# The low half of each split weight chunk, made by a negation and an accumulating transfer

## The chip, the core and the metric

The kernel runs on one core of one Trainium2 chip. The metric is the device time of one execution in microseconds (us). The engines are TensorE (PE in the rows, its weight loads PEld), VectorE (DVE), ScalarE (ACT), GpSimd (POOL) and SyncE (SP, which here issues every transfer); 16 DMA engines move the data.

## The reference, cut to what matters

Two layers of a decoder trunk over 512 tokens of width 1024. Each layer is a token mixer (an input projection, three parallel mixers A, B and C, their projections, sigmoid gates, an output projection), a cross-attention into 256 memory tokens, and a SwiGLU FFN of hidden width 2816, each followed by a LayerNorm of the scaled residual sum:

```python
for l in range(DEPTH):
    h = hybrid_mixer(x, l, w_in[l], ..., w_br_a[l], w_br_b[l], w_br_c[l], w_out[l])
    x = layer_norm(DEEPNORM_ALPHA * x + h, ln1_g[l], ln1_b[l])
    x = layer_norm(DEEPNORM_ALPHA * x + memory_cross_attention(x, mem, xq[l], xkv[l], xo[l]), ...)
    x = layer_norm(DEEPNORM_ALPHA * x + swiglu(x, w_up[l], w_down[l]), ln3_g[l], ln3_b[l])
```

All weights and activations are float32. Nearly all the work is products of activations with the weight matrices.

## The kernel before, in words

**Split products.** A float32 operand w is split into a high part, w rounded to the type float32r (`whi`), and a low part, w minus the high part (`wlo`). A product is three matmuls, high by high, high by low and low by high, added up in PSUM.

**Chunks.** The weights lie in HBM as 372 chunks of 128 x 1024 floats (512 KB), in the order of use. `load_raw` (L254) has SyncE load a chunk into a `raw` tile; `split_chunk` (L262) has ScalarE cast it to `whi` (L267) and notes the subtraction in the list `late`; `flush` (L272) writes the noted subtractions `wlo = raw - whi` (L274), on VectorE for 347 chunks and on GpSimd for the 24 in `on_pool` (the key half of `xkv`, and the first two column tiles of each half of `w_up`), and then loads raw chunks until three more than were split are under way. Chunk 0 is split apart, at the start.

**Steps.** `make_program` lays down 376 steps. A tile step ("a") uses one chunk of 8 x 128 weight columns against all 512 tokens: 24 matmuls. A group ("b") uses several chunks at once for 128 tokens: four steps (two for `xkv`) that share four to six chunks, all of which the group's first step reads one after the other. The main loop (L923) writes, for each step: `refill` (at most two chunks are split, as long as fewer than `pairs` split chunks are live), any chunk of this step that is still unsplit, a `flush` where one is needed, the evacuation of the step before, a piece of the side work (`advance`: attention, recurrence, LayerNorm items), the step's matmuls, and a `flush`. `pairs` is 3 for most tile steps, 5 to 7 for groups and the FFN.

**Order and buffers.** The schedule is manual: every engine works through its instructions in the order in which this loop writes them, and waits on semaphores. `whi`, `wlo`, `raw` and most large activations share 39 slots of 4 KB per partition (`a4`), so a new tile waits for the readers of the tile that had its slot.

**Side work on GpSimd** that this text speaks of: the rotary products (L570, L571), the recurrence's low parts `xl` (L517, L518) and `bl` (L560), its product `ti` (L550), the merges `acc` (L631), and the powers (L376, L477) that give the reciprocal deviations of the norms.

Of the kernel before, what the change touches and what calls it, by code (L numbers as in the profile page):

```python
# [13 lines left out]
AF = mybir.ActivationFunctionType  # L14
ALU = mybir.AluOpType
# [38 lines left out]


def make_program():
    """Order of the matrix products: the weight chunks and the steps that use them.

    A chunk is [128, 1024] floats: (weight, layer, first row tile, row tiles, first column, columns).
    """  # L60
    chunks, steps = [], []

    def ch(name, l, k0, nk, c0, nc_):
# [3 lines left out]
    def tile_step(name, l, c0, act, post, n0=0, n1=S, **kw):  # L67
        c = ch(name, l, 0, KT, c0, P)
        st = Step("a", [c], act=act, post=post, nk=KT, ncol=P, off=0, n0=n0, n1=n1, **kw)
        steps.append(st)  # L70
        return st
# [11 lines left out]
    for l in range(L):  # L83
# [39 lines left out]
        for n in range(KT):  # L123
            st = tile_step("w_in", l, OFF_RX + P * n, "x", ("rx", l, n))
# [49 lines left out]
def kernel(  # L174
# [12 lines left out]
):  # L187
    nc = tc.nc
    chunks, steps = make_program()
    NCH = len(chunks)  # L190

# [10 lines left out]
    def a4(s, shape, dt=F32):  # L202
        return big.tile([P] + shape, dt, tag="a4", name=nm(s), bufs=39)
# [16 lines left out]
    V, A, G, T = nc.vector, nc.scalar, nc.gpsimd, nc.tensor  # L220
# [22 lines left out]
    for s, st in enumerate(steps):  # L243
        for c in st.chunks:
            last_use[c] = s
            if first_use[c] is None:
                first_use[c] = s
    on_pool = {c for c, (name, l, k0, nk, c0, n) in enumerate(chunks)
               if (name == "xkv" and c0 < D) or (name == "w_up" and c0 % HID < 2 * P)}
    raws, hi, lo, late = {}, {}, {}, []  # L250
    ptr = {"raw": 0, "split": 0}
    RAW_AHEAD = 3

    def load_raw():  # L254
        c = ptr["raw"]
        if c >= NCH:
            return
        raws[c] = a4("raw", [1024])
        nc.sync.dma_start(raws[c], wts[c])
        ptr["raw"] += 1  # L260

    def split_chunk(s):  # L262
        c = ptr["split"]
        while ptr["raw"] <= c:
            load_raw()
        h, lw, raw = a4("whi", [1024], F32R), a4("wlo", [1024], F32R), raws.pop(c)
        A.copy(h, raw)  # L267
        hi[c], lo[c] = h, lw
        late.append((lw, raw, h, G if c in on_pool else V))
        ptr["split"] += 1  # L270

    def flush():  # L272
        for lw, raw, h, eng in late:
            eng.tensor_tensor(lw, raw, f(h), ALU.subtract)  # L274
        late.clear()
        while ptr["raw"] < min(NCH, ptr["split"] + RAW_AHEAD):
            load_raw()

    def refill(s, pairs, limit):
        n = 0  # L280
        while ptr["split"] < NCH and n < limit:
            done = sum(1 for c in hi if last_use[c] <= s)
            if len(hi) - done >= pairs:
                break
            split_chunk(min(s, len(steps) - 1))
            n += 1
        for c in [c for c in hi if last_use[c] <= s]:
            del hi[c], lo[c]
# [14 lines left out]
    def met(k):  # L303
        return done.get(k, 0) >= goals.get(k, 1)
# [8 lines left out]
    def advance():  # L313
        for g in list(active):
            if not step_side(g):
                active.remove(g)
        n = 1 if not queue or queue[0][0] != "x" else 4 if len(queue) > 2 else 2
        for _ in range(min(n, len(queue))):
            if queue:
                g = queue.pop(0)[1]  # L320
                if step_side(g):
                    active.append(g)
        active.extend(fresh)
        fresh.clear()
        queue.extend(arriving)
        arriving.clear()
# [537 lines left out]
    for k in range(2):  # L864
        c = slice(512 * k, 512 * (k + 1))
# [8 lines left out]
    def setup_params():  # L874
        nc.sync.dma_start(cols, cols_in.rearrange("l p c -> p l c"))
        lq = t2("lq")
        nc.sync.dma_start(lq, lam_in.partition_broadcast(P))
        for t in range(NT):
            nc.sync.dma_start(x_res[t], x_in[t * P:(t + 1) * P, :])
        for l in range(L):  # L880
            A.activation(hb[:, l, :], cols[:, l, 40:56], AF.Copy, scale=0.5)
            li = 0.8 - 0.6 * math.exp(-0.3 * l)
            V.tensor_scalar(gain[:, l:l + 1], cols[:, l, 64:65], 1.0 - li, None, ALU.mult)
        s1 = small("s1")
        pr = t2("lp")
        for l in range(L):
            o = l * 256
            V.tensor_tensor(pr[:, o:o + 64], lq[:, o:o + 64], lq[:, o + 64:o + 128], ALU.mult)
            V.tensor_tensor(pr[:, o + 64:o + 128], lq[:, o + 128:o + 192], lq[:, o + 192:o + 256],
                            ALU.mult)  # L890
            V.tensor_reduce(s1[:, 2 * l:2 * l + 2],
                            pr[:, o:o + 128].rearrange("p (a b) -> p a b", a=2),
                            axis=AX.X, op=ALU.add)
        A.activation(s1[:, 4:8], s1[:, 0:4], AF.Exp)
        for l in range(L):
            li = 0.8 - 0.6 * math.exp(-0.3 * l)
            V.scalar_tensor_tensor(neglam[:, l:l + 1], s1[:, 5 + 2 * l:6 + 2 * l], -li,
                                   s1[:, 4 + 2 * l:5 + 2 * l], ALU.add, ALU.subtract)

    def setup_decay():  # L900
        s1, e, z, acc = small("s1"), small("e"), small("z"), small("acc")
        lam = cols[:, :, 56:64]
        zz, ee, aa = (t.rearrange("p (l n) -> p l n", l=2) for t in (z, e, acc))
        V.tensor_scalar(zz, lam, -1.0, None, ALU.mult)
        V.tensor_tensor(aa, zz, lam, ALU.max)
        A.activation(e, acc, AF.Exp, scale=-1.0)
        V.tensor_scalar(acc, e, 2.0, None, ALU.add)
        V.reciprocal(acc, acc)
        V.tensor_tensor(e, e, acc, ALU.mult)
        V.tensor_tensor(s1, e, e, ALU.mult)  # L910
        V.tensor_scalar(acc, s1, 1.0 / 21.0, None, ALU.mult)
        for k in range(9, 0, -1):
            V.scalar_tensor_tensor(acc, acc, 1.0 / (2 * k + 1), s1, ALU.add, ALU.mult)
        V.scalar_tensor_tensor(acc, acc, 1.0, e, ALU.add, ALU.mult)
        V.tensor_scalar(z, z, 0.0, 4.0, ALU.max, ALU.mult)
        fl = sp4.rearrange("p l n -> p (l n)")
        V.scalar_tensor_tensor(fl, acc, 8.0, z, ALU.mult, ALU.add)
        V.tensor_scalar(nsp4.rearrange("p l n -> p (l n)"), fl, -1.0, None, ALU.mult)
# [4 lines left out]
    for s, st in enumerate(steps):  # L923
        if s:
            refill(s - 1, steps[s - 1].pairs, 2)
        while ptr["split"] <= max(st.chunks):
            split_chunk(s)
        if late and ptr["split"] - len(late) <= max(st.chunks):
            flush()
        if prev is not None and prev[0].post:  # L930
            POST[prev[0].post[0]](prev[1], *prev[0].post[1:])
        if s == 3:
            setup_params()
        if s == 20:
            setup_decay()
        if st.pre:
            PRE[st.pre[0]](*st.pre[1:])
        credit += prev[0].cost() if prev else 1.0
        if credit > 0.75:
            advance()  # L940
            credit = 0.0
        while not all(met(k) for k in st.need):
            assert active or queue or fresh or arriving, (s, st.need)
            advance()
        prev = (st, emit_main(st))
        flush()
# [26 lines left out]
def _layout(inp):  # L973
    inp = {k: np.asarray(v) for k, v in inp.items()}
    chunks, _ = make_program()
    wts = np.empty((len(chunks), P, 1024), np.float32)
    for i, (name, l, k0, nk, c0, ncol) in enumerate(chunks):
# [46 lines left out]
```

## Time and profile before

| | us |
|---|---|
| median of 2 runs (2271.61 to 2272.38) | 2271.99 |
| the profiled execution: its span | 2272.3 |
| PE busy | 2238.5 (99%) |
| DVE busy | 1267.1 (56%) |
| ACT busy | 898.3 (40%) |
| POOL busy | 351.6 (15%) |
| DMA: share of 16 engines' span, transfers by SP | 29.5% |

The span runs from the first instruction to the last on the core. A PE row lasts longer than its place in the stream, since matmuls overlap: a 128x512 one is shown with 0.39 us and the next starts 0.23 us later, so the busy share alone doesn't tell how full the stream is. The waits say that: idle time of an engine by what ended it. PEclk is the TensorE clock granted in a stretch, as a share of full speed.

### The profile page before, as it was taken

The numbers are of one execution on the slowest core, as the hardware profiler recorded it, in microseconds if no ns is written. First come the engines' busy times: TensorE is split into PE (matmuls) and PEld (weight loads), VectorE is DVE, ScalarE is ACT, GpSimd is POOL, SyncE is SP. The second block draws the span as 40 slices with busy tenths as digits, with TensorE's granted clock in tenths as the row PEclk, the third lists the DMA queues.
The fourth block names the chain that finished last, engine by engine and source line by source line (L and its number), as shares of the span: only waits on it lengthen the run. The fifth ranks groups of instructions, "written<-read, shape, count | busy, mean of one in ns | idle before, by whom it ended". The sixth has DMA issues, their size and how long they took to land.

```text
span 2272.3 us, 26789 instructions
## 1 busy us (share of the span) xinstructions
PE 2238.5 (99%) x10516; PEld 1821.5 (80%) x10516; DVE 1267.1 (56%) x2058; ACT 898.3 (40%) x1583; POOL 351.6 (15%) x238
## 2 busy tenths in 40 slices
PE   9999999999999999999999999999999999999998
PEld 7778777778888888888887777777788888888887
DVE  6656766646655743243566476666467457332434
ACT  5444466644244332122134445666432342221330
POOL 2202213320300300000022031133203003000000
PEclk9999999999999999999999999999999999999999
DMA  7122323234332222142231222232343323222321
GB/s 269 63 65 76 101 66 97 93 98 166 102 112 102 93 91 86 66 147 100 81 126 56 65 75 93 65 107 84 116 148 105 110 101 103 85 82 97 125 93 38
DMA packets 65278, 224.37 MB, mean 99 GB/s; under 512 B 7936, under 2 KB 7936, under 8 KB 65152
## 3 DMA queue, kind: packets, MB, share of 16 engines
q1 hardware_dynamic: 65152, 222.66, 29.5%
q8 instruction: 83, 1.36, 0.2%
q14 instruction: 43, 0.35, 0.0%
HBM read 212.14 MB, written 2.10 MB: 94 GB/s over the span
## 4 chain that ended last, share of the span: by engine, by line
PE 72%; issue 17%; DVE 5%; POOL 3%; ACT 2%; DMA 0%; SPq 0%; POOLq 0%; ACTq 0%
PE ps L810 17%; PE ps L811 17%; PE ps L812 17%; PE ps L839 5%; PE ps L841 5%; PE ps L840 5%; POOL wlo L274 2%; PE sc L341 2%; PE o L414 1%; PE sc L340 1%; DVE x L482 1%; POOL ln L477 1%; PE tp L408 1%; PE o L370 1%; ACT whi L267 1%
## 5 line engine op out<-in xcount | busy, mean ns | idle before, releaser
L810 PE MATMUL ps<-xh,whi 128*128 128x512 f32 (+1 forms) x1792 | 697.3, 389 | 2.9 <-ACT xh L868 1.7
L811 PE MATMUL ps<-xl,whi 128*128 128x512 f32 (+1 forms) x1792 | 689.1, 385 | 0.8 <-DVE xl L754 0.5
L812 PE MATMUL ps<-xh,wlo 128*128 128x512 f32 (+1 forms) x1792 | 688.2, 384 | 1.3 <-POOL wlo L274 1.3
L274 DVE TENSOR_TENSOR wlo<-raw,whi 128x1024 fp32r<-128x1024 f32 x347 | 447.3, 1303 | 47.7 <-ACT whi L267 40.2
L267 ACT CAST whi<-raw 128x1024 fp32r<-128x1024 f32 x371 | 382.7, 1046 | 148.9 <-PE ps L840 97.8
L810 PEld LDWEIGHTS ps<-xh,whi 128*128 128x128 f32 x1792 | 339.4, 189 | 80.7 <-issue 6.5
L812 PEld LDWEIGHTS ps<-xh,wlo 128*128 128x128 f32 x1792 | 339.2, 189 | 68.9 <-POOL wlo L274 2.1
L811 PEld LDWEIGHTS ps<-xl,whi 128*128 128x128 f32 x1792 | 339.5, 189 | 66.1 <-DVE xl L869 1.0
L477 POOL TENSOR_TENSOR ln<-ln,expo 128x1 f32<-128x1 f32 x24 | 34.4, 1434 | 1082.9 <-DVE ln L476 1082.9
L839 PE MATMUL ps<-whi,hh 128*128 128x512 f32 x352 | 137.1, 389 | 0.0
L841 PE MATMUL ps<-whi,hl 128*128 128x512 f32 x352 | 137.0, 389 | 0.0
L840 PE MATMUL ps<-wlo,hh 128*128 128x512 f32 x352 | 136.9, 389 | 0.0
L744 ACT CAST hh<-fg 128x512 fp32r<-128x512 f32 x44 | 27.3, 620 | 191.8 <-DVE fg L743 191.8
L501 ACT CAST xh<-tp 128x256 fp32r<-128x256 f32 x80 | 28.0, 376 | 178.4 <-PE tp L495 101.2
L733 DVE SCALAR_TENSOR_TENSOR fg<-fg,ps 128x512 f32<-128x512 f32 x44 | 30.3, 688 | 116.9 <-ACT fg L732 116.9
L743 DVE TENSOR_TENSOR fg<-fg,ps 128x512 f32<-128x512 f32 x44 | 30.3, 688 | 114.4 <-PE ps L812 114.4
L570 POOL TENSOR_TENSOR raw<-raw,tabs 128x512 f32<-128x512 f32 x32 | 42.6, 1332 | 250.6 <-ACT raw L567 250.6
L732 ACT ACTIVATE fg<-ps 128x512 f32<-128x512 f32 x44 | 26.3, 598 | 135.2 <-PE ps L812 135.2
L680 DVE SCALAR_TENSOR_TENSOR x<-ps,x 128x512 f32<-128x512 f32 x48 | 33.0, 686 | 80.5 <-PE ps L841 80.4
L274 POOL TENSOR_TENSOR wlo<-raw,whi 128x1024 fp32r<-128x1024 f32 x24 | 63.5, 2661 | 88.4 <-ACT whi L267 88.4
L840 PEld LDWEIGHTS ps<-wlo,hh 128*128 128x128 f32 x352 | 66.1, 188 | 13.7
L839 PEld LDWEIGHTS ps<-whi,hh 128*128 128x128 f32 x352 | 66.1, 188 | 13.7
(233 smaller groups left out, 3576.6 us busy)
## 6 DMA issues: line engine op xcount, KB each, us to landing
raw<-in_wts_dram SPq DMA_DIRECT2D x371, 512.0 KB, 3.6
xs<-xs SPq DMA_DIRECT2D x32, 128.0 KB, 2.2
lng<-in_lnp_in_dram SPq DMA_DIRECT2D x6, 512.0 KB, 4.7
lnb<-in_lnp_in_dram SPq DMA_DIRECT2D x6, 512.0 KB, 5.0
tabs<-in_tabs_in_dram SPq DMA_DIRECT2D x4, 512.0 KB, 8.5
x<-in_x_in_dram SPq DMA_DIRECT2D x4, 512.0 KB, 9.3
qkA<-qkA SPq DMA_DIRECT2D x16, 128.0 KB, 2.2
qkC<-qkC SPq DMA_DIRECT2D x16, 128.0 KB, 2.2
```

Source lines behind the costliest of these rows:

```text
L267: A.copy(h, raw)
L274: eng.tensor_tensor(lw, raw, f(h), ALU.subtract)
L341: T.matmul(sc[:, :w], ql[r, i * P:(i + 1) * P], kk[r, c, :w], start=False, stop=True)
L477: G.tensor_tensor(st[:, 15:16], st[:, 14:15], expo, ALU.pow)
L570: G.tensor_tensor(raw, raw, tab[:, 0, :], ALU.mult)
L680: V.scalar_tensor_tensor(xs, ps, co, xs, ALU.mult, ALU.add)
L810: T.matmul(pv, wh, xh, start=(kt == 0), stop=False)
L811: T.matmul(pv, wh, xl, start=False, stop=False)
L812: T.matmul(pv, wl, xh, start=False, stop=(kt == st.nk - 1))
L839: T.matmul(ps, xh, wh, start=(i == 0), stop=False)
L840: T.matmul(ps, xh, wl, start=False, stop=False)
L841: T.matmul(ps, xl, wh, start=False, stop=(i == n - 1))
```

## The change

For every chunk but the first eight and the 24 in `on_pool`, the subtraction on VectorE goes. In its place ScalarE writes the negated raw chunk, rounded to float32r, into `wlo` (which is -`whi`, as the rounding is symmetric), and GpSimd issues a transfer that reads the chunk once more from HBM and adds it to `wlo` in SBUF. Both are written in `split_chunk`, right behind the cast, so they stand ahead of what the loop writes next. The subtractions that stay go through `late` as before, but any that is noted is flushed in the same step, before the step's matmuls. The blank lines replace a docstring and shift later lines by four.

```diff
@@ -266,8 +266,12 @@
         h, lw, raw = a4("whi", [1024], F32R), a4("wlo", [1024], F32R), raws.pop(c)
         A.copy(h, raw)
         hi[c], lo[c] = h, lw
-        late.append((lw, raw, h, G if c in on_pool else V))
         ptr["split"] += 1
+        if c < 8 or c in on_pool:
+            late.append((lw, raw, h, G if c in on_pool else V))
+        else:
+            A.activation(lw, raw, AF.Copy, scale=-1.0)
+            nc.gpsimd.dma_start(lw, wts[c], accum_op=ALU.add)
@@ -925,7 +929,7 @@
         while ptr["split"] <= max(st.chunks):
             split_chunk(s)
-        if late and ptr["split"] - len(late) <= max(st.chunks):
+        if late:
             flush()
```

Counted over the program, VectorE loses 340 instructions, ScalarE gains 340 and GpSimd 340 transfers; TensorE's and SyncE's instructions are as many as before.

ScalarE, where the chunks of the first `w_out` group of layer 0 are split (`mh` is the high part of the merged branches, `mkh` of the memory keys). Before:

```order
L267 CAST whi_4507<-raw_4433 128x1024
L638 CAST mh_4475<-acc_2211 128x512
L267 CAST whi_4542<-raw_4468 128x1024
L267 CAST whi_4545<-raw_4505 128x1024
L707 CAST mkh_4548<-ps_4514 128x256
L267 CAST whi_4585<-raw_4540 128x1024
```

and now:

```order
L267 CAST whi_4579<-raw_4505 128x1024
L273 ACTIVATE wlo_4580<-raw_4505 128x1024
L642 CAST mh_4550<-acc_2240 128x512
L267 CAST whi_4615<-raw_4511 128x1024
L273 ACTIVATE wlo_4616<-raw_4511 128x1024
L267 CAST whi_4620<-raw_4546 128x1024
L273 ACTIVATE wlo_4621<-raw_4546 128x1024
L711 CAST mkh_4625<-ps_4588 128x256
L267 CAST whi_4660<-raw_4613 128x1024
L273 ACTIVATE wlo_4661<-raw_4613 128x1024
```

Each cast of a chunk is followed by its negation, and the casts behind it stand one instruction later for each.

GpSimd, at the last recurrence item of layer 0 that TensorE waits for (`xl` is the low part of its convolved input). Before:

```order
L631 TENSOR_TENSOR acc_2211<-acc_2211,g_3598 128x512 x2
L560 TENSOR_TENSOR bl_3340<-m_3522,bh_3339 128x512 x2
L517 TENSOR_TENSOR xl_3916<-xc_3809,xs_3874 64x512
L518 TENSOR_TENSOR xl_3916<-xc_3809,xs_3874 64x512
```

and now:

```order
L274 DMA wlo_3915<-in_wts_dram 128x1024
L635 TENSOR_TENSOR acc_2240<-acc_2240,g_3651 128x512
L274 DMA wlo_3967<-in_wts_dram 128x1024
L635 TENSOR_TENSOR acc_2240<-acc_2240,g_3651 128x512
L564 TENSOR_TENSOR bl_3387<-m_3573,bh_3386 128x512 x2
L521 TENSOR_TENSOR xl_3976<-xc_3867,xs_3933 64x512
L522 TENSOR_TENSOR xl_3976<-xc_3867,xs_3933 64x512
```

A transfer stands ahead of each merge, so the low parts behind them come after two transfers that wait for ScalarE's negations.

GpSimd, at the LayerNorm behind `w_out` of layer 0 (L477, now L481, are its powers; the subtractions are those of `xkv`). Before:

```order
L477 TENSOR_TENSOR ln_4624<-ln_4624,expo 128x1
L274 TENSOR_TENSOR wlo_4759<-raw_4724,whi_4758 128x1024
L477 TENSOR_TENSOR ln_4656<-ln_4656,expo 128x1
L477 TENSOR_TENSOR ln_4684<-ln_4684,expo 128x1
L477 TENSOR_TENSOR ln_4730<-ln_4730,expo 128x1
L274 TENSOR_TENSOR wlo_4861<-raw_4726,whi_4860 128x1024
L274 TENSOR_TENSOR wlo_4864<-raw_4728,whi_4863 128x1024
```

and now:

```order
L274 DMA wlo_4800<-in_wts_dram 128x1024
L278 TENSOR_TENSOR wlo_4839<-raw_4832,whi_4838 128x1024
L481 TENSOR_TENSOR ln_4701<-ln_4701,expo 128x1
L481 TENSOR_TENSOR ln_4733<-ln_4733,expo 128x1
L481 TENSOR_TENSOR ln_4761<-ln_4761,expo 128x1
L278 TENSOR_TENSOR wlo_4941<-raw_4834,whi_4940 128x1024
L278 TENSOR_TENSOR wlo_4944<-raw_4836,whi_4943 128x1024
L481 TENSOR_TENSOR ln_4804<-ln_4804,expo 128x1
```

The subtractions have moved ahead of the first and of the fourth power.

## Rows read from the trace of the kernel before

**Rows 1.** The page's head and its list of busy times.
```profile
span 2272.3 us, 26789 instructions
PE 2238.5 (99%) x10516; PEld 1821.5 (80%) x10516; DVE 1267.1 (56%) x2058; ACT 898.3 (40%) x1583; POOL 351.6 (15%) x238
```

**Rows 2.** Waits of PE: us in total, times, longest us.
```profile
PE z L525 <- POOL xl L517: 5.4, 2, 2.7
PE ps L812 <- POOL wlo L274: 5.1, 6, 1.9
PE tp L364 <- DVE pr L359: 4.4, 3, 3.3
PE tp L495 <- DVE x L482: 3.1, 2, 1.5
...
PE ps L811 <- DVE xl L869: 0.2, 1, 0.2
```

**Rows 3.** Groups by line: busy us, mean ns of one, idle before and releasers.
```profile
L274 DVE TENSOR_TENSOR wlo<-raw,whi 128x1024 fp32r<-128x1024 f32 x347 | 447.3, 1303 | 47.7 <-ACT whi L267 40.2 <-PE ps L841 7.4
L267 ACT CAST whi<-raw 128x1024 fp32r<-128x1024 f32 x371 | 382.7, 1046 | 148.9 <-PE ps L840 97.8 <-DVE wlo L274 26.8 <-DMA raw<-in_wts_dram 23.5
L546 ACT ACTIVATE m<-m 128x1024 f32<-128x1024 f32 x8 | 8.5, 1061 | 0.1
L570 POOL TENSOR_TENSOR raw<-raw,tabs 128x512 f32<-128x512 f32 x32 | 42.6, 1332 | 250.6 <-ACT raw L567 250.6
L274 POOL TENSOR_TENSOR wlo<-raw,whi 128x1024 fp32r<-128x1024 f32 x24 | 63.5, 2661 | 88.4 <-ACT whi L267 88.4
```

**Rows 4.** DMA queues; issues by line with KB each and median us to landing.
```profile
q1 hardware_dynamic: 65152, 222.66, 29.5%
raw<-in_wts_dram SPq DMA_DIRECT2D x371, 512.0 KB, 3.6
```

**Rows 5.** Timeline of SP: one issue (start us, us).
```profile
60.13 0.33 SPq L259 DMA_DIRECT2D raw<-in_wts_dram  x1
```

**Rows 6.** Stretches: PE, PEld, DVE, ACT, POOL busy, PEclk, DMA share, GB/s.
```profile
985.00:1078.00 93.00, 93.00 (x412) 77.02 (x411) 37.66 (x43) 26.42 (x34) 0.00 (x0) 1.00 0.28 96
555.00:575.00 20.00, 20.00 (x112) 17.52 (x112) 11.28 (x14) 8.97 (x12) 0.00 (x0) 1.00 0.60 210
618.00:648.00 30.00, 30.00 (x171) 26.36 (x171) 19.07 (x28) 15.95 (x28) 3.27 (x2) 1.00 0.42 141
1134.00:1148.00 14.00, 14.00 (x72) 11.76 (x71) 10.81 (x16) 6.30 (x13) 1.52 (x1) 1.00 0.65 235
466.00:476.00 10.00, 7.28 (x17) 4.79 (x17) 3.64 (x4) 4.35 (x6) 4.10 (x3) 0.66 0.42 134
```

**Rows 7.** Timeline of ACT: casts for the first `w_out` group.
```profile
554.07 1.05 ACT L267 CAST whi<-raw 128x1024 fp32r<-128x1024 f32 x1
...
556.99 1.99 ACT L267 CAST whi<-raw 128x1024 fp32r<-128x1024 f32 x2
558.88 0.36 ACT L707 CAST mkh<-ps 128x256 fp32r<-128x256 f32 x1
559.15 2.00 ACT L267 CAST whi<-raw 128x1024 fp32r<-128x1024 f32 x2
```

**Rows 8.** Timeline of PE: first use of that group's first and fourth `wlo`.
```profile
560.80 0.40 PE L840 MATMUL ps<-wlo,mh 128*128 128x512 f32 x1
...
564.90 0.39 PE L840 MATMUL ps<-wlo,mh 128*128 128x512 f32 x1
```

**Rows 9.** Timeline of ACT: casts for the second `xkv` value group.
```profile
633.16 2.95 ACT L267 CAST whi<-raw 128x1024 fp32r<-128x1024 f32 x3
```

**Rows 10.** Timeline of PE: first use of that group's fourth `wlo`.
```profile
642.23 0.39 PE L840 MATMUL ps<-wlo,mh 128*128 128x512 f32 x1
```

**Rows 11.** Timeline of ACT: last two casts for layer 1's first group.
```profile
1133.44 2.00 ACT L267 CAST whi<-raw 128x1024 fp32r<-128x1024 f32 x2
```

**Rows 12.** Timeline of PE: first use of that group's fourth `wlo`.
```profile
1139.55 0.39 PE L840 MATMUL ps<-wlo,xh 128*128 128x512 f32 x1
```

**Rows 13.** Timeline of ACT and POOL before the last recurrence item; PE's wait.
```profile
460.43 1.06 ACT L267 CAST whi<-raw 128x1024 fp32r<-128x1024 f32 x1
...
461.31 1.67 POOL L631 TENSOR_TENSOR acc<-acc,g 128x512 f32<-128x512 f32 x1 [1.09 <-DVE g L630]
...
468.89 0.79 PE L525 MATMUL z<-xl,gw 64*128 64x512 f32 x1 [2.72 <-POOL xl L517]
```

## The prediction

> **What bounds the kernel now.** I began with the head of the page and the busy times [rows 1]: TensorE is busy for 99% of a span of 2272.3 us, VectorE for 56%, ScalarE for 40%, GpSimd for 15%. A busy TensorE need not have a full stream, so the list of its waits came second [rows 2]. It has twelve entries, of which the first four and the last are shown, and they add up to 25.3 us. In the FFN the stream is simply full: 412 matmuls in 93.00 us are 0.226 us each [rows 6], and a tile step of 24 takes 5.42 us. So this kernel is bound by TensorE's stream, and what the change takes off VectorE, 340 subtractions at 1.303 us or 443 us [rows 3], lies almost wholly beside it. The ceiling of any gain is the 25.3 us of waits plus what half-speed stretches behind them cost. One of these shows in the ten microseconds from 466: TensorE waited 2.72 us [rows 13], then the granted clock averaged 0.66, that is, it had fallen from 2.4 to 1.2 GHz for 6.8 us, which costs 3.4 us of stream. The longest waits in the rows are 3.3 us, twice 2.7 us and 1.9 us [rows 2]; were all four followed by such a stretch, that is 14 us, so the ceiling is near 39 us, 1.7% of the span. About 2%, or 45 us, is what I take a measurement to tell from no change, so faster by that much is practically excluded.
>
> What can be lost is another matter, since `wlo` now comes later. The question is where a chunk's cast ends only a few microseconds before TensorE first reads its `wlo`.
>
> **The new path, step by step.** Before, `wlo` follows its cast by one subtraction of 1.30 us on an engine that is free half the time. Now:
> - The negation on ScalarE: 1.06 us, by the 128x1024 activation with a scale [rows 3]. 340 of them are 361 us, which lifts ScalarE to 55%. In a burst each cast also waits for the negations ahead of it.
> - The issue on GpSimd. The trace has none. Below, SyncE's 0.33 us [rows 5]; above, GpSimd's longest instruction, 2.66 us [rows 3]. I take 1.3 us, the mean of its short product [rows 3], as the price of one instruction on that engine. 340 of them are 442 us, GpSimd 35% busy.
> - From issue to landing. A raw load of the same 512 KB lands after 3.6 us (median) [rows 4]; that is the lower end. The DMA engines' time for one load is 0.295 x 2272.3 us x 0.524 MB / 222.66 MB = 1.58 us [rows 1, 4]. The accumulate must read the old `wlo` too, one more pass of the same bytes, so 5.2 us is the upper end. I take the middle, 4.4 us.
> - The DMA engines' time for one accumulate: 1.58 us at least, 3.16 us if the second read costs as much as the first. I take 2.0 us, nearer the plain load, since only the read from SBUF is new. 340 of them add 680 us to the 670 us now used, 59% of the span.
>
> Cast to landing is then 1.06 + 1.3 + 4.4 = 6.8 us. In a tile stage with three live pairs a chunk is split two steps ahead, about 10.8 us; in the FFN with six pairs, five steps, 27 us. Both cover 6.8 us, and per step of 5.42 us the DMA engines do 1.58 + 2.0 us. So the bulk of the chunks costs nothing; the cover is gone only if the accumulate holds the engines for more than 5.42 - 1.58 = 3.84 us.
>
> The bursts are different: a group's first step reads all its chunks in 5.4 us.
> - `w_out`, once per layer. Before, the four casts start at 554.07, 556.99 (two) and 559.15 [rows 7], the reads of the first and fourth `wlo` at 560.80 and 564.90 [rows 8]. With negations between them the fourth negation ends near 563.3. Plus 1.3 + 4.4 us is 569.0, 4.1 us late. The DMA engines are 60% busy in this stretch [rows 6]; four accumulates are 8 us, and about 6 us of loads come between, so from 557.5 the fourth lands near 572: 7 us late. Bounds: 563.3 + 0.33 + 3.6 is 2.3 us late; four at 3.16 us behind 8 us of loads, 15 us late.
> - The `xkv` value groups, once per layer, eight chunks for two token steps each. The last three casts start at 633.16 [rows 9]; with negations they end near 639.5, plus 5.7 is 645.2 against the read at 642.23 [rows 10]: 3 us. Eight accumulates are 16 us and the loads 42% of 30 us [rows 6], together 28.6 us where some 25 us are to be had: 3 us more, so 6. Bounds: 1 and 14 us.
> - Layer 1's first group. Two casts start at 1133.44 [rows 11]; the second negation ends at 1137.7, plus 5.7 is 1143.4 against 1139.55 [rows 12]: 4 us. Bounds 2 and, with engines 65% busy [rows 6], 9 us.
>
> Together 2 x (7 + 6) + 4 = 30 us, between 9 and 67. Some of these waits are as long as the 2.72 us behind which the clock fell; five more such stretches at 2 us net (half of 3.4 us and a little more, since at half speed the late chunk catches up) are 10 us, between 0 and 17.
>
> **What else moves.** GpSimd's queue gets a transfer ahead of each merge. Before the last recurrence item, the cast ends at 461.49 and its negation now at 462.5, while the merge behind the transfer started at 461.31 [rows 13]: 1.2 us of blocking and 1.3 us of issue, which delay `xl`, for which TensorE already waits. Twice, 5 us; between 0 and 10. Earlier items are blocked too, but TensorE doesn't wait for them.
>
> On the other side, subtractions of `on_pool` chunks now stand ahead of powers that wait for VectorE, so the 5.1 us that TensorE waits for `wlo` of GpSimd [rows 2] should mostly go. A VectorE with 443 us less to do should end most of the 4.4 us for `pr` [rows 2]. I take 9 us off, between 5 and the whole 39.
>
> The sum: 30 + 10 + 5 - 9 = +36 us on the profiled span of 2272.3 us, which is 0.3 us from the median of the runs: **2308 us**, 1.6% slower.
>
> **Rivals.** *The accumulate takes the engines twice as long as a load.* A result needs two reads, and if the two take turns it costs 3.16 us: then the bursts queue, and the places above are at their upper ends. 67 + 17 + 10 - 5 = +89 us, 2361 us, slower by 4%. It decides from about 2.3 us per accumulate, where the sum passes 45 us. For it speaks that loads already fill 42 to 65% of the bursts [rows 6]; against it that the second read is of SBUF and not of HBM. The Trainium skill's page "Collectives: The Full Stack", section "The bandwidth ceiling: the fold count and why AG ≠ RS ≠ AR", says that a reducing step is half as fast as a plain copy, because two source reads go through the same ring. No run shown so far has an accumulating transfer, so the trace neither agrees nor disagrees; by that rule the sum would be this rival's 2361 us.
>
> *The DMA engines become the bound.* From 3.84 us per accumulate the tile stages fall behind too. At 6 us each step of 5.42 us would need 7.6 us; over 340 chunks some 740 us, so about 3010 us, and at 4.5 us some 225 us, about 2500. Nothing in the trace shows such a price, only that the operation is unknown.
>
> *It is all hidden, and VectorE's relief shows.* If the transfers land within the bounds' lower ends, 9 us of bursts stand against 9 us or more of relief: 2272 us, and down to 2250 if most waits and half-speed stretches go. For it: most chunks have 10 us or more of lead. Against it: in the bursts even the lower ends are late.
>
> **Chances.** My forecast, bursts late by some tens of microseconds but within 2%: 0.45. Engines twice as long: 0.32. DMA-bound: 0.10. Hidden: 0.13. So faster by over 2% 0.01, within 2% 0.57, slower 0.42. The range leaves out the DMA-bound case and the better half of the hidden one: 2260 to 2375.
>
> **What would show it.** In the changed profile, TensorE should wait for transfers into `wlo` at L844 (`w_out`, `xkv` values, layer 1's first group) and hardly at L816; the waits for GpSimd's `wlo` should be gone and that for `xl` be longer. The row of the accumulates gives issue, landing and engine share: about 1.3 us, 4.4 us and 2.0 us. TensorE waiting for `wlo` in the FFN, or a DMA share far above 60%, would make the forecast wrong towards slower; no waits at the bursts, towards no change.

## The result and the profile after

The changed kernel takes 2387.28 us (median of two runs, 2381.02 and 2393.55) against 2271.99: a ratio of 1.0505, 95% interval 1.0475 to 1.0534. It is slower by 5%. The two runs lie 12.5 us apart with granted clocks of 0.977 and 0.970, and the trace is of the shorter one: the accounts below are of its 107 us, while the medians differ by 115. The forecast was 2308 and the range ended at 2375, so the time lies beyond it, on the side of the rival in which an accumulate takes the engines twice as long.

First the page's head, its DMA queues and its rows of DMA issues, for the profiled run of 2381.02 us. They answer to [rows 1, 4].

```profile
span 2379.2 us, 27760 instructions
PE 2272.6 (96%) x10516; PEld 1837.0 (77%) x10516; DVE 862.9 (36%) x1718; ACT 1219.0 (51%) x1923; POOL 612.7 (26%) x578
...
q0 software_dynamic: 48960, 178.28, 42.2%
q1 hardware_dynamic: 65152, 222.66, 27.6%
...
raw<-in_wts_dram SPq DMA_DIRECT2D x371, 512.0 KB, 5.5
...
wlo<-in_wts_dram POOLq DMA_DIRECT2D x340, 512.0 KB, 7.3
```

The last row is the new operation: an accumulate of 512 KB lands 7.3 us after its issue, where I had taken 4.4 and held 5.2 for the most. The queue q0 carries nothing but these 340 transfers, so each holds the 16 DMA engines for 0.422 x 2379.2 / 340 = 2.95 us, where I had taken 2.0. The raw loads suffer with it: 5.5 us instead of 3.6.

Next TensorE's waits, which answer to [rows 2]; the columns are the same.

```profile
PE ps L844 <- DMA wlo<-in_wts_dram: 60.9, 27, 6.6
PE tp L368 <- DVE pr L363: 10.5, 5, 4.1
PE z L529 <- POOL xl L521: 5.4, 2, 2.7
...
PE z L528 <- DMA xs<-xs: 3.9, 2, 2.0
...
PE ps L816 <- POOL wlo L278: 2.7, 2, 1.3
```

One new row heads the list, at the line that the forecast named: 27 waits at L844 for a transfer into `wlo`, 60.9 us. The fifteen rows of the list come to 98.1 us, 72.8 more than before. The rest is clock. The mean granted clock fell from 0.991 to 0.977; the time that this costs, span times the missing share, rose from 0.009 x 2272.3 = 20.5 to 0.023 x 2379.2 = 54.7 us, by 34. Together that is 107 us, and the span grew by 106.9. The clocks are rounded to 0.001, or 2 us of span, so the match is in part luck; but no other loss of more than a few microseconds is left. TensorE stands, and after standing it runs slowly for a while.

The groups by line, which answer to [rows 3]:

```profile
L267 ACT CAST whi<-raw 128x1024 fp32r<-128x1024 f32 x371 | 385.9, 1042 | 47.1 <-DMA raw<-in_wts_dram 43.5 <-PE ps L845 2.7
L273 ACT ACTIVATE wlo<-raw 128x1024 fp32r<-128x1024 f32 x340 | 358.9, 1056 | 84.3 <-PE ps L844 84.3
L274 POOL DMA_DIRECT2D wlo<-in_wts_dram x340 | 296.6, 872 | 1424.1 <-ACT wlo L273 1266.4 <-PE ps L816 36.4 <-PE ps L845 18.9
```

The negation costs 1.056 us, as taken. The issue costs 0.87 us on GpSimd, less than the 1.3 taken. The long idle time before L274 is GpSimd waiting at the head of its queue for negations: 1266 us in which nothing behind the transfer ran there.

**One burst read through.** The window row of `w_out` in [rows 6] becomes three; the later rows are the second `xkv` value group and a stretch of the FFN.

```profile
556.00:566.00 10.00, 10.00 (x67) 9.22 (x66) 4.04 (x5) 6.40 (x8) 2.48 (x3) 1.00 0.84 237
566.00:576.00 10.00, 5.12 (x17) 3.10 (x15) 0.85 (x2) 10.00 (x13) 4.33 (x5) 0.83 1.05 280
576.00:586.00 10.00, 5.70 (x25) 4.40 (x25) 1.39 (x2) 1.60 (x2) 1.21 (x2) 1.00 1.06 277
660.00:670.00 10.00, 3.91 (x12) 2.30 (x10) 0.69 (x1) 2.62 (x4) 1.75 (x2) 0.77 1.03 267
...
1000.00:1110.00 110.00, 110.00 (x487) 91.12 (x486) 18.62 (x27) 51.42 (x60) 18.95 (x22) 1.00 0.87 212
```

In the bursts the DMA share (the column before the last) is at its ceiling and TensorE is busy for half the time. In the stretch of the FFN the share is 0.87 and TensorE never stands: 1.58 + 2.95 = 4.53 us of engine time for each step of 5.42 us, which is 0.84. So the load is not the trouble where it is even; it is where several chunks are needed at once. GpSimd's timeline and then TensorE's in that burst (start, duration, idle time before it):

```profile
560.19 0.89 POOL L274 DMA_DIRECT2D wlo<-in_wts_dram  x1 [3.46 <-ACT wlo L273]
564.96 0.86 POOL L274 DMA_DIRECT2D wlo<-in_wts_dram  x1 [3.88 <-ACT wlo L273]
566.85 0.86 POOL L274 DMA_DIRECT2D wlo<-in_wts_dram  x1 [1.02 <-ACT mkh L711]
569.01 0.86 POOL L274 DMA_DIRECT2D wlo<-in_wts_dram  x1 [1.29 <-ACT wlo L273]
```

```profile
569.74 0.69 PE L844 MATMUL ps<-wlo,mh 128*128 128x512 f32 x1 [3.11 <-DMA wlo<-in_wts_dram]
570.23 0.63 PE L845 MATMUL ps<-whi,ml 128*128 128x512 f32 x1
...
574.34 0.51 PE L844 MATMUL ps<-wlo,mh 128*128 128x512 f32 x1 [1.78 <-DMA wlo<-in_wts_dram]
...
578.11 0.50 PE L844 MATMUL ps<-wlo,mh 128*128 128x512 f32 x1 [2.10 <-DMA wlo<-in_wts_dram]
...
581.96 0.50 PE L844 MATMUL ps<-wlo,mh 128*128 128x512 f32 x1 [2.20 <-DMA wlo<-in_wts_dram]
```

The four transfers are issued 1.9 to 4.8 us apart, but their first readers stand 3.8 to 4.6 us apart: each `wlo` keeps TensorE waiting anew, where the forecast saw one wait that grows to 7 us at the fourth. The DMA view of the stretch from 556 to 580 says why: there an accumulate takes 13.8 us to land, a raw load 15.0. The loads, those of two LayerNorm parameters among them, hold 54.0% of the engines' time, the accumulates 42.0%.

```profile
q1 hardware_dynamic: 1161, 4.26, 54.0%
q0 software_dynamic: 536, 2.00, 42.0%
...
raw<-in_wts_dram SPq DMA_DIRECT2D x8, 512.0 KB, 15.0
wlo<-in_wts_dram POOLq DMA_DIRECT2D x8, 512.0 KB, 13.8
```

**Where the 107 us arose.** The end of each TensorE step, after minus before, was read from TensorE's instructions in both traces; its growth is summed over the steps of a place (layer 0 / layer 1):

| place | us |
|---|---|
| first `w_out` group | +11.5 / +12.0 |
| `xkv` value groups | +17.5 / +17.6 |
| second `w_down` group of the first FFN half | +10.7 / +11.4 |
| layer 1's first group | +9.7 |
| first mixer's attention | +5.1 / +11.9 |
| recurrence input stage, the one step that lost | +2.2 / +2.2 |
| start of `w_up` | +1.3 / +2.8 |
| everything else (what is left of 106.9) | -9.0 |

The first four places are the bursts: 90 us of the 107 (89 in the expectations below, which were read in another way). The loss of the recurrence's input stage has its row above: two waits of TensorE, 3.9 us, for the copies `xs<-xs` between partitions, which carry the high part of its input. They landed after 2.2 to 2.4 us before and take up to 6.3 us now.

### The profile page after: what moved, and what is told of

Its sections match the earlier page's. It is cut to its first block, busy times and chain, and to the rows that moved or that the text cites. A ratio compares the mean times of both kernels' runs of the same rounds, so it can differ in the third digit from the quotient of the medians.

```text
span 2379.2 us, 27760 instructions
## 1 busy us (share of the span) xinstructions
PE 2272.6 (96%) x10516; PEld 1837.0 (77%) x10516; DVE 862.9 (36%) x1718; ACT 1219.0 (51%) x1923; POOL 612.7 (26%) x578
## 4 chain that ended last, share of the span: by engine, by line
PE 63%; issue 19%; POOL 5%; DMA 4%; DVE 4%; ACT 4%; POOLq 0%; SPq 0%; ACTq 0%; DVEq 0%
PE ps L814 13%; PE ps L815 13%; PE ps L816 13%; PE ps L844 5%; PE ps L845 4%; PE ps L843 4%; DMA wlo<-in_wts_dram 3%; POOL wlo L274 2%; PE sc L345 2%; POOL wlo L278 1%; PE sc L344 1%; PE o L418 1%; ACT wlo L273 1%; ACT whi L267 1%; PE tp L412 1%
## 5 line engine op out<-in xcount | busy, mean ns | idle before, releaser
L816 PE MATMUL ps<-xh,wlo 128*128 128x512 f32 (+1 forms) x1792 | 689.1, 385 | 0.0
L274 POOL DMA_DIRECT2D wlo<-in_wts_dram x340 | 296.6, 872 | 1424.1 <-ACT wlo L273 1266.4
L273 ACT ACTIVATE wlo<-raw 128x1024 fp32r<-128x1024 f32 x340 | 358.9, 1056 | 84.3 <-PE ps L844 84.3
L816 PEld LDWEIGHTS ps<-xh,wlo 128*128 128x128 f32 x1792 | 340.0, 190 | 66.8
L844 PE MATMUL ps<-wlo,hh 128*128 128x512 f32 x352 | 139.7, 397 | 16.0 <-DMA wlo<-in_wts_dram 16.0
L844 PE MATMUL ps<-wlo,mh 128*128 128x512 f32 x192 | 83.2, 433 | 38.1 <-DMA wlo<-in_wts_dram 38.1
L844 PEld LDWEIGHTS ps<-wlo,hh 128*128 128x128 f32 x352 | 67.1, 191 | 32.6 <-DMA wlo<-in_wts_dram 18.8
L844 PEld LDWEIGHTS ps<-wlo,mh 128*128 128x128 f32 x192 | 39.1, 204 | 56.4 <-DMA wlo<-in_wts_dram 48.8
L843 PE MATMUL ps<-whi,mh 128*128 128x512 f32 x192 | 80.7, 420 | 0.0
L845 PE MATMUL ps<-whi,ml 128*128 128x512 f32 x192 | 80.4, 419 | 0.0
```

The source lines that it names most:

```text
L273: A.activation(lw, raw, AF.Copy, scale=-1.0)
L274: nc.gpsimd.dma_start(lw, wts[c], accum_op=ALU.add)
L816: T.matmul(pv, wl, xh, start=False, stop=(kt == st.nk - 1))
L843: T.matmul(ps, xh, wh, start=(i == 0), stop=False)
L844: T.matmul(ps, xh, wl, start=False, stop=False)
L845: T.matmul(ps, xl, wh, start=False, stop=(i == n - 1))
```

## The experiments

The theory, A: an accumulate costs only where TensorE reads the chunk before the transfer has landed, that is in the bursts, and there by its distance to landing and by the engine time that it adds. Its rivals: the negations load ScalarE; the blocked queue of GpSimd does it; the transfers slow TensorE wherever they run; or the changed condition for the flush does it. In the diffs below, lines not shown are those of the changed kernel unless the kernel before is named.

**e1: the burst chunks back on VectorE.**

```
+    def in_burst(c):
+        name, l, k0, nk, c0, n = chunks[c]
+        return ((name == "w_out" and c0 == 0) or (name == "xkv" and c0 >= D)
+                or (name == "w_down" and k0 < GROUPS[1][0] and c0 > 0)
+                or (name == "w_in" and l == 1 and c0 == OFF_AV))
...
-        if c < 8 or c in on_pool:
+        if c < 8 or c in on_pool or in_burst(c):
```

> The changed kernel, but the 36 chunks of the bursts (first w_out group and the xkv value groups of each layer, second w_down group of each layer's first half, layer 1's first group) keep the subtraction on VectorE. Theory A (the accumulates land too late in the bursts, nowhere else): the stretches of those groups gave 89 of the 107 us, so about 2300 us, and TensorE's waits for transfers into wlo fall from 60.9 us to under 10. Theory B (GpSimd and ScalarE work through longer queues, and everything behind them is late): 36 of 340 chunks change little, 2360 us or more.

Measured: 2295.18 us, ratio 1.0100 [1.0071, 1.0129]. Forty of the 340 chunks (the trace has 300 transfers; the expectation counted 36) carry 92 of the 115 us between the medians, and 86 of the 107 between the profiled runs. The four bursts lose nothing any more. Transfers still land only after 7.1 us and still hold 38.8% of the engines, but TensorE's list of waits now reads:

```profile
PE tp L374 <- DVE pr L369: 11.1, 5, 4.1
PE z L535 <- POOL xl L527: 5.4, 2, 2.7
...
PE ps L822 <- DMA wlo<-in_wts_dram: 1.2, 2, 0.6
```

The wait for transfers is gone but for 1.2 us. The 20 us that remain sit in the attention, the recurrence's input stage and the start of `w_up`.

**e2: no transfer, VectorE adds the raw weights to the negated high part.**

```
-            nc.gpsimd.dma_start(lw, wts[c], accum_op=ALU.add)
+            late.append((lw, raw, lw, V))
...
-            eng.tensor_tensor(lw, raw, f(h), ALU.subtract)
+            eng.tensor_tensor(lw, raw, f(h), ALU.add if h is lw else ALU.subtract)
```

> The changed kernel without its transfers: ScalarE still writes the negated chunk, VectorE adds the raw chunk to it. Theory A: the transfers are all of the loss, 2265 to 2285 us. Theory B in the form that ScalarE's 340 negations (361 us) are to blame: most of the loss stays, 2330 us or more.

Measured: 2324.88 us, 1.0231 [1.0201, 1.0260]. Missed. The additions wait in VectorE's queue for negations on ScalarE, and what stands behind them is late: TensorE waits 13.8 us for `pr`, 13.1 for `xl`, 6.9 for `ti`. This kernel did not only take the transfer away; it put another chain in its place, in which VectorE waits 571.9 us for negations. n1 below is the cleaner cut.

**e3: a plain transfer instead of the accumulating one.**

```
-            nc.gpsimd.dma_start(lw, wts[c], accum_op=ALU.add)
+            nc.gpsimd.dma_start(lw, wts[c])
```

> The changed kernel with plain transfers in place of the accumulating ones (same chunk, same issue; wlo is overwritten, so the low part is left out of the result). Theory A in the form that the second read of the accumulate makes it long: 1.6 us of the DMA engines each instead of 2.95, landing after about 5 us instead of 7.3, half of the loss gone, about 2320 us. In the form that the issue by GpSimd and the plain distance to the landing do it: little change, 2365 us or more.

Measured: 2339.87 us, 1.0297 [1.0267, 1.0327], between the two. Rows of its page and of its waits:

```profile
q0 software_dynamic: 48960, 178.28, 24.1%
...
wlo<-in_wts_dram POOLq DMA_DIRECT2D x340, 512.0 KB, 4.5
```

```profile
PE ps L844 <- DMA wlo<-in_wts_dram: 35.3, 18, 6.0
```

The same bytes without the addition land after 4.5 us and cost 0.241 x 2337.2 / 340 = 1.66 us of the engines. So what the accumulate costs over a copy is 1.29 us of engine time and, with the load that this makes, 2.8 us of landing. In the bursts (step ends as in the table above) the loss is 47 us instead of 90.

**e4: the kernel before with the new condition of the flush alone** (`if late:`).

> The kernel before with the new flush condition alone. As predicted: GpSimd's subtractions stand ahead of the powers, TensorE's 5.1 us of waits for them mostly go, 2266 to 2270 us. Rival: all of VectorE's subtractions move ahead of the evacuations of PSUM too and delay them, 2272 us or slower.

Measured: 2286.28 us, 1.0061 [1.0038, 1.0083]. Missed by some 18 us. Flushing whenever something is pending puts VectorE's 340 subtractions ahead of side work that TensorE waits for: `xl` costs 8.8 us instead of 5.4 and `pr` 8.2 instead of 4.4. The wait for GpSimd's `wlo` does fall, from 5.1 to 2.7, and the step ends gain 0.5 and 2.1 us at the key half of `xkv` and 1.8 per layer at `xo`, as in the changed kernel, while the start of `w_up` loses 1.8 per layer. So these gains, and most of that loss, come of the flush and not of the transfers.

**n1: negations, but no transfers.**

```
-            nc.gpsimd.dma_start(lw, wts[c], accum_op=ALU.add)
```

> The changed kernel without its transfers and with nothing in their place: ScalarE writes the negated chunk, and that stays as the low part, so the raw weights are not added to it. What is left is ScalarE's 361 us of negations and the flush condition. Theory A: the transfers made the waits in the bursts, and the rest of the loss (some 18 us, in the stage of mixer A's attention and behind) is ScalarE's: about 2285 us. If the loss of the run in which VectorE added the raw chunk (52 us) was ScalarE's and not VectorE's waiting for it: 2315 us or more.

Measured: 2272.69 us, 0.9998 [0.9986, 1.0009]. This misses the forecast of about 2285 too. The bursts lose 0.0 us, so ScalarE's 359 us of negations make nothing of the loss there, which ends that rival. Over the whole kernel the zero is a balance: the negations and the flush against the relief of VectorE, with 9.7 us lost in the first mixer's attention and 6.9 gained where TensorE waited for `xl`. Two rows of TensorE's waits:

```profile
PE tp L367 <- DVE pr L362: 8.1, 3, 3.4
...
PE z L528 <- POOL xl L520: 1.6, 2, 0.8
```

Here VectorE has 37% to do and GpSimd's queue holds no transfer, and the wait for `xl` falls from 5.4 to 1.6 us. In the changed kernel, which differs only by the transfers, it is 5.4. So there is a relief at that place, and the transfers take it back. The wait for `pr`, in contrast, grows without any transfer.

**n2: the transfer carries an eighth of the columns.**

```
-            nc.gpsimd.dma_start(lw, wts[c], accum_op=ALU.add)
+            nc.gpsimd.dma_start(lw[:, :128], wts[c, :, :128], accum_op=ALU.add)
```

> The changed kernel with transfers of only the first 128 of 1024 columns of each chunk (the other columns of wlo lack the raw weights). GpSimd issues as many transfers and waits for as many negations, but 64 KB move instead of 512. Theory A (what the transfers move and when it lands): landing after 3 us or less, burst waits mostly gone, 2285 to 2305 us. Theory B (GpSimd's queue, blocked by waits for negations and lengthened by issues): the loss stays, 2350 us or more.

Measured: 2328.18 us, 1.0246 [1.0217, 1.0276], between the two. Its transfers land after 2.8 us and hold the engines for 0.080 x 2328.0 / 340 = 0.55 us; TensorE still waits for them:

```profile
PE ps L844 <- DMA wlo<-in_wts_dram: 21.1, 11, 4.3
```

The bursts lose 34 us, over a third of their loss, with an eighth of the bytes. GpSimd's queue is not what makes them late there: in the changed kernel a transfer is issued 0.3 us after its negation ends (median of 340). At the first `w_out` group even these small transfers land only after 6.4 us (565 to 575 us in this run's trace), where loads hold 87.8% of the engines. The plain copy of all bytes (e3) costs the bursts 13 us more than this run, and the addition on top of it another 43; the first of these steps changes two things at once, the bytes and the addition.

**n3: the negation on VectorE.**

```
-            A.activation(lw, raw, AF.Copy, scale=-1.0)
+            V.tensor_scalar(lw, f(h), -1.0, None, ALU.mult)
```

> The changed kernel with the negation (of the high part) on VectorE instead of ScalarE. Theory A: the bursts stay late, so most of the loss stays; of the some 18 us in the attention stage of mixer A half or more comes back if ScalarE's negations made it: 2365 to 2375 us. If ScalarE has no part in it: 2385 us or more, since VectorE's shorter queue was the only relief.

Measured: 2404.22 us, 1.0581 [1.0550, 1.0612], worse than the changed kernel and in the range of the second branch. The attention loses 15 us against 17, so little of it came back. The four bursts lose 88 us, as before; what is new is the second `w_out` group, 7 us per layer, where the negations in VectorE's queue end 28 us after their casts (median of eight) instead of 1, and the recurrence, 5.5 us per layer. TensorE waits 73.9 us for transfers, 40 times.

**n4: in the bursts the chunks are split three pairs earlier.**

```
-            if len(hi) - done >= pairs:
+            if len(hi) - done >= pairs + (3 if in_burst(ptr["split"]) else 0):
```

> The changed kernel, with up to three more split chunks live while the next chunk to split belongs to one of the bursts, so that these are split one or more steps earlier. Nothing else moves. Theory A (lead against landing time): the 89 us of the bursts halve, about 2340 us. Rival (the DMA engines are too busy there for any lead, or the slots come free too late): 2370 us or more.

Measured: 2345.40 us, 1.0322 [1.0292, 1.0352]. Near the forecast.

```profile
PE ps L850 <- DMA wlo<-in_wts_dram: 38.5, 22, 3.9
```

With the accumulate's price unchanged (7.3 us, 42.5% of the engines), more lead alone takes 42 us off the median and 35 off the profiled run; the bursts go from 90 to 55 us, which is not quite the half that was expected. Layer 1's first group loses nothing any more; `w_out` loses 6.7 and 6.9, the `xkv` groups still 11.6 and 11.8, and the second `w_down` groups 10.9 and 7.4.

**h1: transfers for the 80 `w_up` chunks alone.** From the kernel before, whose order of the flush is kept:

```
-        late.append((lw, raw, h, G if c in on_pool else V))
+        if chunks[c][0] != "w_up" or c in on_pool:
+            late.append((lw, raw, h, G if c in on_pool else V, c))
+        else:
+            A.activation(lw, raw, AF.Copy, scale=-1.0)
+            nc.gpsimd.dma_start(lw, wts[c], accum_op=ALU.add)
...
-        if late and ptr["split"] - len(late) <= max(st.chunks):
+        if late and late[0][4] <= max(st.chunks):
```

> Only the 80 w_up chunks that VectorE served go by negation and transfer; all others stay as in the kernel before, in their old order. Theory A (a transfer costs only where TensorE reads the chunk before it has landed, and where its engine's queue is needed): in the FFN a chunk is split some 25 us ahead and GpSimd has nothing else to do, so no wait for a transfer and 2272 us, within 5. Rival (accumulates slow the loads or TensorE's stream itself, wherever they run): the 80 cost their share of the 107 us, about 25 us, so 2297.

Measured: 2273.09 us, 1.0000 [0.9991, 1.0010]. Hit. The stretch of the FFN, and the row of the transfers:

```profile
1000.00:1100.00 100.00, 100.00 (x443) 82.83 (x442) 28.11 (x37) 35.34 (x43) 6.97 (x9) 1.00 0.60 155
```

```profile
wlo<-in_wts_dram POOLq DMA_DIRECT2D x80, 512.0 KB, 7.4
```

An accumulate lands as late here as anywhere, after 7.4 us (13.7 at most), and is free: the casts of these 80 chunks end 15 to 35 us before TensorE's first use, 30 in the median. That ends the rival by which transfers slow TensorE wherever they run.

**h2: e1, with the rotary products on VectorE.** What is left in e1's attention had its clue in the trace of the changed kernel. First GpSimd, then VectorE, then TensorE around the wait of 4.07 us in layer 1:

```profile
1257.06 0.89 POOL L274 DMA_DIRECT2D wlo<-in_wts_dram  x1 [6.36 <-ACT wlo L273]
1257.67 1.60 POOL L574 TENSOR_TENSOR raw<-raw,tabs 128x512 f32<-128x512 f32 x1
1258.92 1.56 POOL L575 TENSOR_TENSOR sh<-sh,tabs 128x512 f32<-128x512 f32 x1
```

```profile
1258.05 2.99 DVE L591 TENSOR_TENSOR qkA<-raw,qkA 64x512 fp32r<-64x512 f32 x1
1261.05 0.69 DVE L592 TENSOR_TENSOR qkA<-raw,qkA 64x512 fp32r<-64x512 f32 x1
...
1262.41 0.35 DVE L363 SCALAR_TENSOR_TENSOR pr<-pr,st,pr 128x128 f32<-128x128 f32 x1
```

```profile
1262.82 0.47 PE L368 MATMUL tp<-ident,pr 128*128 128x128 f32 x1 [4.07 <-DVE pr L363]
```

The transfer waits 6.36 us for its negation; the two products behind it run right after it, and just then VectorE starts a subtraction that takes 2.99 us instead of the 0.69 of its twin. It ends 0.56 us after the second product. The softmax's division, for which TensorE waits, stands behind it.

How much of this is new, the trace of the kernel before tells. The two subtractions in all their eight places, minimum, median and maximum in ns, before and then in the changed kernel, and TensorE's wait of before at this place:

```profile
L587 DVE TENSOR_TENSOR qkA<-raw,qkA x8: 684/1074/1105, 40.9 to 1232.5; 64x512 fp32r<-64x512 f32 x8
L588 DVE TENSOR_TENSOR qkA<-raw,qkA x8: 686/1660/1685, 42.0 to 1233.2; 64x512 fp32r<-64x512 f32 x8
...
L591 DVE TENSOR_TENSOR qkA<-raw,qkA x8: 685/2952/3025, 44.7 to 1296.9; 64x512 fp32r<-64x512 f32 x8
L592 DVE TENSOR_TENSOR qkA<-raw,qkA x8: 686/687/689, 47.7 to 1297.6; 64x512 fp32r<-64x512 f32 x8
```

```profile
1202.14 0.33 PE L364 MATMUL tp<-ident,pr 128*128 128x128 f32 x1 [3.29 <-DVE pr L359]
```

In both kernels five of the eight pairs meet the products. Such a pair takes 2.8 us before and 3.6 to 3.7 now, 1.4 where it meets none. So the transfers lengthen a collision that was there, by 0.9 us, and 3.29 of the 4.07 us at this place are old. The expectations of h2 and v2 take the collision for new, and for rare in the kernel before; the rows don't bear that out.

```
-        G.tensor_tensor(raw, raw, tab[:, 0, :], ALU.mult)
-        G.tensor_tensor(sh, sh, tab[:, 1, :], ALU.mult)
+        V.tensor_tensor(raw, raw, tab[:, 0, :], ALU.mult)
+        V.tensor_tensor(sh, sh, tab[:, 1, :], ALU.mult)
```

> As e1 (the burst chunks back on VectorE, the others by transfer), and the two products of the rotary embedding, which stand behind a transfer in GpSimd's queue, are issued by VectorE. Theory (in the first mixer's attention the transfers push these products to where VectorE's subtractions for qkA run; those then take 2.95 us instead of 1.07, and the softmax's pr, for which TensorE waits, stands behind them): the subtractions fall to 0.69 us, the waits for pr from 11.1 us towards 6, the time from 2295 to about 2285. Rival (the softmax is late because of ScalarE's negations, or VectorE with 64 products more is as late): pr's waits stay at 11 us or more, 2295 to 2305.

Measured: 2288.27 us, 1.0074 [1.0059, 1.0089]. The subtraction's row (minimum, median and maximum in ns) and TensorE's wait:

```profile
L597 DVE TENSOR_TENSOR qkA<-raw,qkA x8: 684/685/686, 43.9 to 1244.4; 64x512 fp32r<-64x512 f32 x8
```

```profile
PE tp L374 <- DVE pr L369: 7.4, 4, 2.8
```

All eight are at 0.69 us, and the wait for `pr` fell from 11.1 to 7.4 us. The intervals of e1 and h2 overlap, so the 7 us between their medians are not shown by the times alone; the rows show that the subtractions stand behind those waits. The move takes away the old part of the collision with the new one, so it doesn't tell what the transfers added.

**v1 and v2: the kernel before, mended.** v1 moves one subtraction behind `xl` from GpSimd to VectorE, v2 also the rotary products.

```
-            G.tensor_tensor(dl, m, f(dh), ALU.subtract)
+            V.tensor_tensor(dl, m, f(dh), ALU.subtract)
```

> The kernel before, with the one subtraction that makes the low part of the recurrence's output (xl's partner, dl at L560) on VectorE instead of GpSimd; no transfers. If it is GpSimd's queue for which TensorE waits there, the two waits of 2.7 us and the 3.4 us of half-speed stretch behind each go: 12 us less, 2260. Rival (VectorE's queue is as late at that point, as it was where its subtractions were moved ahead): the waits stay in another name, 2268 to 2280.

> The kernel before with the low part of the recurrence's output and the two rotary products on VectorE, no transfers. Theory: before, the products rarely meet those subtractions (1.07 us median against 0.69), so little is to be had: 2258 to 2263. Rival: VectorE, with 443 us of weight subtractions, is late with the products: slower than v1_xl_vector, 2266 to 2275.

Measured: v1 2262.56 us, 0.9954 [0.9937, 0.9970]; v2 2261.58 us, 0.9949 [0.9932, 0.9965], which can't be told from v1. Both are half a per cent faster than the kernel before, without any of the change, and near their forecasts; in v1 the waits for `xl` are gone from TensorE's list. The stretch of [rows 13] in v1:

```profile
466.00:476.00 10.00, 10.00 (x42) 7.46 (x41) 6.60 (x7) 7.99 (x12) 0.84 (x1) 1.00 0.47 147
```

TensorE is busy for all of it at a clock of 1.00, where it was 7.28 of 10 us at 0.66 [rows 6].

## Why the prediction was wrong

**The step that failed is the price of the accumulate**, where I took "the middle, 4.4 us" to landing, and 2.0 us of the engines "nearer the plain load, since only the read from SBUF is new". It lands after 7.3 us, beyond the upper bound of 5.2, and takes 2.95 us, near the upper bound of 3.16. What was taken for the most, a load's landing of 3.6 us and one more pass of the bytes, is the least: of the 340 the quickest lands after 5.2 us, the slowest after 19.1. That price had no term for queueing, though the loads themselves went up to 5.5 us under the new traffic. On engine time the rival's price was right: 2.95 against 1.66 us of the same transfer without the addition (e3), 1.78 times as long. That two reads make it so is not shown: q0 has as many packets and bytes in both runs, and the packets take longer. The Trainium skill's page "Collectives: The Full Stack", section "The bandwidth ceiling: the fold count and why AG ≠ RS ≠ AR", states half the rate of a copy for the reducing step of a collective; by that rule this transfer would have held the engines twice as long as the copy, against the 1.78 times measured.

**The mechanism held.** TensorE waits at L844 for transfers, not at L816; the tile stages and the `w_up` chunks hide their transfers (h1: 1.0000); the DMA-bound rival, which needed 3.84 us per accumulate, did not come, and the FFN's share of 0.87 shows how near it was.

**The terms.**
- Bursts: 14 us forecast for `w_out`, 12 for `xkv`, 4 for layer 1's first group; with the 10 us for the clock that is 40 for these three. The step ends show 23.5 + 35.2 + 9.7 = 68.4, clock included. The `xkv` value groups are furthest off, 17.6 per layer against 6: each has four chunks for two steps. In `w_out` the sum had 8 us of accumulates and 6 of loads on the engines; the 24 us from 556 hold 10.1 and 13.0. (Its upper bound there is off too: 557.5 + 8 + 4 x 3.16 is 578, 13 us late and not 15.)
- A fourth kind of burst was not named at all, the second `w_down` group of the first FFN half: 22.1 us. I had put all of the FFN under six live pairs with 27 us of lead. The trace of the kernel before could have told: the casts of this group's last three chunks end 5.8 and 2.2 us before TensorE's first product of the group and 0.3 us behind it, after waits for raw loads.
- The clock: 10 us forecast, 17 at most; the mean clocks above give 34. I had assumed five stretches behind waits; there are 27 waits for transfers.
- GpSimd's queue before `xl`: 5 us more forecast; the wait is 5.4 as before. But n1 shows 1.6 without transfers, so against that state they do cost about 4 us.
- The gains: 9 us forecast, and -9.0 is what the table leaves. That the two agree is luck: `wlo` of GpSimd went from 5.1 to 2.7 and not to nothing, by the flush (e4), and `pr` was not relieved at all.
- Not foreseen: `pr`, which was to be relieved (4.4 us), costs 10.5. The step ends show 17 us at the attention. Most of the growth of the waits comes without any transfer: they are 8.1 us in n1 and 8.2 with the flush alone (e4). The rest fits the collision of VectorE with GpSimd's products, which the transfers lengthen; no run separates it.

The rival of 2361 us had the right price of engine time and still fell 26 us short, by the `w_down` groups (22.1) and the clock (34 against its 17), less what else differs. No run was aimed at the recurrence's input stage; that the copies `xs<-xs` land late because the transfers and loads fill the engines fits n1, where the latest lands after 2.6 us and TensorE doesn't wait for them, but is not shown by itself.

## What to carry to other kernels

A transfer that adds in place is neither a copy nor a vector operation: here it took 1.78 copies of engine time, so price it at nearly two, and count from the cast to the landing through every queue on the way, at the load of that place and not at the median. Then look for the places where several chunks are needed at once rather than at the mean DMA share; with lead it is free (h1), without it each chunk can make TensorE wait anew, and the clock added half as much again (34 us to 72.8 of waits). A transfer issued from an engine that also computes held that engine until its input was ready (6.36 us in one place) and kept the work behind it waiting. And a change that only moves instructions can cost as much as one expects to gain: the new flush condition alone cost 14 us (e4).

## What the runs showed of the hardware

- An accumulate of 512 KB from HBM into SBUF, issued by GpSimd: 0.87 us to issue, 7.3 us to landing (median; 5.2 to 19.1), 2.95 us of 16 engines. The same as a plain copy (e3): 4.5 and 1.66 us. Of 64 KB, accumulating (n2): 2.8 and 0.55 us.
- A VectorE subtraction of two SBUF tensors, 64x512, took 0.69 us alone and 2.95 to 3.03 us in the five of eight places of the changed kernel where it met two GpSimd products. The Trainium skill's "SBUF — State Buffer", section "SBUF: two separate sides", says that such an operation and one of GpSimd share a port pair, which one of them holds for the whole instruction. The trace agrees: the subtraction ended 0.56 us after the second product, about what it takes alone. It does not bear the rule out for every GpSimd instruction: beside a power on 128x1 (L380 of the changed kernel, near 1297 us), recorded as running at the same time, it took 0.69 us too.
- After a wait of 3.11 us a 512-column product's record lasted 0.63 to 0.69 us instead of 0.39, and the ten microseconds averaged a granted clock of 0.83, between the levels of 1.2 and 2.4 GHz.
